# Two chains of two heads in place of one chain of four, in the gated recurrence of block 2

## The chip, the cores and the metric

The kernel runs on one core of a Trainium2 chip. The metric is the device time of one execution in microseconds (us), the median over runs. Engines are named as in the profile: PE is TensorE's matmuls, PEld its weight loads, DVE is VectorE, ACT is ScalarE, POOL is GpSimd, SP the engine whose queue issues the plain DMAs.

## The reference

One sequence of 256 tokens, width 1024, float32. First two "hybrid" layers (block 1), then two layers of block 2, each made of a feed-forward part, a mixer and a second feed-forward part, all with RMS norms and residuals. The mixer of block 2 has a forgetting attention (4 heads), a dilated attention (4 heads) and a gated linear recurrence (HGRN, 4 heads with 128 key and 128 value channels each), whose outputs are concatenated and projected by `w_out_2`. The change touches only the recurrence. For one head, with forget gate f between 0 and 1 per key channel, key k = 1 - f, query q (a SiLU of its projection) and value v:

```python
S[t] = diag(f[t]) @ S[t-1] + outer(k[t], v[t])     # 128 x 128 state
o[t] = S[t].T @ q[t]
y    = rmsnorm(o) * silu(gate)                     # gate: the hg columns
```

so that o[t] is the sum over s <= t of v[s] times the sum over channels of q[t] k[s] exp(sum of log f over s+1..t).

## The kernel before

**Layout.** Activations are kept with channels on partitions and the 256 tokens in the free dimension. The dense products are done in three terms: each weight chunk (128 x 2048 float32, 1 MB) is loaded to a tile `st` by SP's queue (`weight_loads`, line 600), its rounded part `hi` is made on ScalarE and the remainder `lo` on VectorE, or on ScalarE and a GpSimd accumulating DMA (`weight_splits`, line 617); a dense group of 256 output columns (`dense_t`, line 660) is then 48 matmuls of 128 x 256. There are three tiles each of `st`, `hi` and `lo`.

**Order.** No loop order is written by hand. Every piece of work is a generator that yields operations; at build time the `Scheduler` (lines 258 to 397) keeps one modelled clock per engine and always issues the operation with the smallest (modelled start - priority x weight). Each engine then runs its instructions in that fixed order. A generator that yields a tuple of tags waits until tiles of those tags are free: `lev` (3 tiles), `u` (3), `sm` (4 PSUM banks), `acc` (4 PSUM banks for dense groups). Priorities are in `PRIO`: attention 1.8, recurrence 2.3, a level's products 0.3, evacuation of dense groups 1.1. The model gives a ScalarE operation on SBUF 0.093 us plus 0.833 ns per column (line 454).

**The mixer of block 2** (`mix_b`, line 1370) runs twice. Dense groups follow `ORDER_B` (line 35): after the values `hi`, they are fv, hf0, hq0, hf1, fk, hq1, fq, dv, dk, dq, hg0, hg1. A digit 0 or 1 means heads 0 and 1, or heads 2 and 3. `hf` and `hq` evacuate a group into `sp` (running sums of log f, two halves of 1024 columns: prefix and suffix sides) and `kq` (keys and queries); `log1p_exp` (line 1403) is their common part and works in a `lev` tile. `hg` does the same for the output gate, then waits for the event `o0` or `o1` of its two heads and writes K blocks 4 and 5 (heads 0, 1) or 6 and 7 (heads 2, 3) of the projection's input.

**The recurrence** (`recurrence`, line 1512) is done without a loop over tokens. It waits for hf0, hf1, hq0 and hq1, takes the diagonal, and then goes through eight levels m = 1, 2, 4, ... 128. At each level ScalarE exponentiates the mixed halves of `sp` into a `lev` tile (1024 columns: 4 heads x 256 tokens), VectorE doubles the span of the running sums (two adds of 512 columns, line 1527 and 1528; not at the last level), and a spawned `level` task multiplies by `kq`, takes an `sm` bank, runs 64-column products on TensorE (`blocks`, line 1461) and merges them by a predicated copy into `at` (line 1489), or by ScalarE copies for the upper levels. Levels merge in order. After the eighth, for heads 0, 1 and then 2, 3: products of the values with `at`, square, product with ones for the norm, logarithm, and the event `o0` or `o1`.

**The projection** (`out_proj`, line 731): four banks are open at once. For each of the first four column blocks it runs K blocks 0 to 5, then K blocks 6 and 7 of the four (`LATE_B = 2`, `OPEN = 4`); the last four column blocks run straight through. K blocks 0 and 1 are the forgetting attention, 2 and 3 the dilated one. One K block is a pair: a 512-column matmul (line 576) and a 256-column one (line 577). An attention half (`heads`, line 963) takes two `sm` banks at once and there are two halves.

Of the kernel before, what the change touches and what calls it, by code (L numbers as in the profile page):

```python
# [17 lines left out]
P = 128  # L18
# [381 lines left out]
class Builder:  # L400
# [969 lines left out]
    def mix_b(self, l, st, nxt):  # L1370
        nc, tc, s = self.nc, self.tc, self.s
        done = Event()
        with tc.tile_pool(name="mixb", bufs=1, reuse_waits="tile") as mp:
# [29 lines left out]
            def log1p_exp(ps, nch, cols=None):  # L1403

                e = yield ("lev",)
                a = e[:, :nch * 512].rearrange("p (n f t) -> p n f t", n=nch, f=2)
                yield self.A(a[:, 0], ps, AF.Abs)
                if nch == 2:
                    for j in range(2):
                        yield self.A(a[:, 1, j], ps[:, j], AF.Abs, bias=cols[:, j:j + 1])  # L1410
                flat = e[:, :nch * 512]
                yield self.A(flat, flat, AF.Exp, scale=-1.0)
                yield self.A(flat, flat, AF.Ln, bias=1.0)
                return e, a

            def hf(c):
                def f_(bank, ps):
                    yield self.bconsts
                    h0 = 4 * l + 2 * c
                    e, a = yield from log1p_exp(ps, 2, self.nlncol[:, h0:h0 + 2])  # L1420
                    u, t1 = yield ("u", "u")
                    yield self.stt(u, ps, 0.0, a[:, 0], ALU.max, ALU.add)
                    yield self.stt(t1, ps, 0.0, a[:, 0], ALU.min, ALU.subtract)
                    for j in range(2):
                        h = 2 * c + j
# [5 lines left out]
                    yield self.V("tensor_tensor", u, u, a[:, 1], op=ALU.subtract)  # L1431
                    s.put("lev", e)
                    yield self.V("tensor_tensor", sp_[:, 1, c * 512:c * 512 + 512].rearrange("p (a b) -> p a b", a=2),
                                  t1, u, op=ALU.subtract)
                    s.put("u", u)
                    s.put("u", t1)
                    E[f"hf{c}"].done = True
                return f_

            def hq(c):  # L1440
                def f_(bank, ps):
                    e, a = yield from log1p_exp(ps, 1)
                    u = yield ("u",)
                    yield self.stt(u, ps, 0.0, a[:, 0], ALU.min, ALU.subtract)
                    s.put("lev", e)
                    yield self.A(u, u, AF.Exp)
                    yield self.tt(kq[:, 1, c * 512:c * 512 + 512].rearrange("p (a b) -> p a b", a=2), ps, u, ALU.mult)
                    s.put("u", u)
                    s.put("acc", bank)
                    E[f"hq{c}"].done = True  # L1450
                return f_

            def mixed(tl, m):

                return bass.AP(tensor=tl.tensor, offset=tl.offset,
                               ap=[list(tl.ap[0]), [2 * m, D // (2 * m)], [D + m, 2], [1, m]])

            b8 = lambda bank: bank.rearrange("p (h t) -> p h t", h=8)
            atc = at[:, 2].rearrange("p h (b j) -> p (h b) j", b=2)

            def blocks(bank, t, left, right):

                ops = []
                for h in range(4):
                    for b in range(2):
                        q = slice(h * T + t * P + 64 * b, h * T + t * P + 64 * b + 64)
                        ops.append((b8(bank)[64 * b:64 * b + 64, 4 * t + h], left[:, q], right[:, q], True, True))
                return self.MMs(ops)

            def diagonal():  # L1470
                bank = yield ("sm",)
                for t in range(2):
                    yield blocks(bank, t, kq[:, 0], kq[:, 1])
                yield self.tt(atc, b8(bank), self.c["identc"][:, None, :].to_broadcast([P, 8, 64]), ALU.mult)
                s.put("sm", bank)
                box["lev"] = [Event() for _ in range(9)]
                box["lev"][0].done = True

            def level(lev, e):
                m = 1 << lev  # L1480
                ev = e.rearrange("p (b two m) -> p b two m", two=2, m=m)
                yield self.V("tensor_tensor", ev, ev, mixed(kq, m), op=ALU.mult)
                bank = yield ("sm",)
                if m < 64:
                    for t in range(2):
                        yield blocks(bank, t, e, e)
                    yield box["lev"][lev]
                    mk = self.msk[:, lev * 64:lev * 64 + 64][:, None, :].to_broadcast([P, 8, 64])
                    yield Op([("V", .602, lambda: self.nc.vector.copy_predicated(atc, mk, b8(bank)))],
                             [extent(atc)], [extent(bank), extent(self.msk)])  # L1490
                    if m == 32:
                        for b in range(2):
                            bs = slice(64 * b, 64 * b + 64)
                            yield self.A(at[bs, 0:2, :, bs], atc[bs].rearrange("p (t h) j -> p t h j", t=2), AF.Copy)
                elif m == 64:
                    for h in range(4):
                        yield self.MMs([(b8(bank)[64 * t:64 * t + 64, h], e[:, h * T + t * P:h * T + t * P + 64],
                                         e[:, h * T + t * P + 64:h * T + t * P + P], True, True) for t in range(2)])
                    yield box["lev"][lev]
                    for t in range(2):  # L1500
                        yield self.A(at[:64, t, :, 64:], b8(bank)[64 * t:64 * t + 64, :4], AF.Copy)
                else:
                    pa = bank.rearrange("p (h t) -> p h t", h=4)
                    for h in range(4):
                        yield self.MM(pa[:, h], e[:, h * T:h * T + P], e[:, h * T + P:h * T + T])
                    yield box["lev"][lev]
                    yield self.A(at[:, 2], pa, AF.Copy)
                s.put("sm", bank)
                s.put("lev", e)
                box["lev"][lev + 1].done = True  # L1510

            def recurrence():

                for n in ("hf0", "hf1", "hq0", "hq1", "S0"):
                    yield E[n]
                yield from diagonal()
                for lev in range(8):
# [3 lines left out]
                    yield self.A(ev, mixed(sp_, m), AF.Exp)  # L1521
                    s.spawn(level(lev, e), PRIO["level"])
                    if m < 128:
                        sl = sp_[:, 0].rearrange("p (b two m) -> p b two m", two=2, m=m)
                        pl = sp_[:, 1].rearrange("p (b two m) -> p b two m", two=2, m=m)
                        n = D // (2 * m)
                        yield self.tt(sl[:, :, 0], sl[:, :, 0], pl[:, :, 1, m - 1:m].to_broadcast([P, n, m]), ALU.add)
                        yield self.tt(pl[:, :, 1], pl[:, :, 1], pl[:, :, 0, m - 1:m].to_broadcast([P, n, m]), ALU.add)
                yield box["lev"][8]
                for c in range(2):  # L1530
                    bank, sq = yield ("sm", "u")
                    po = bank.rearrange("p (a t) -> p a t", a=2)
                    for j in range(2):
                        h = 2 * c + j
                        vs = slice(h * P, h * P + P)
                        yield self.MM(po[:, j, :P], hv[:, 0, vs], at[:, 0, h])
                        yield self.MM(po[:, j, P:], hv[:, 0, vs], at[:, 2, h], True, False)
                        yield self.MM(po[:, j, P:], hv[:, 1, vs], at[:, 1, h], False, True)
                    yield self.A(sq, po, AF.Square)
                    yield self.A(oh[:, 2 * c:2 * c + 2], po, AF.Copy)  # L1540
                    yield self.MM(po, self.ones, sq)
                    s.put("u", sq)
                    yield self.A(lr[:, 2 * c:2 * c + 2], po, AF.Ln, scale=1.0 / P, bias=self.epsc)
                    s.put("sm", bank)
                    E[f"o{c}"].done = True
# [98 lines left out]
            def hg(c):  # L1644
                def f_(bank, ps):
                    e, a = yield from log1p_exp(ps, 1)
                    w = yield ("u",)
                    yield self.stt(w, ps, 0.0, a[:, 0], ALU.min, ALU.subtract)
# [52 lines left out]
            s.spawn(recurrence(), PRIO["rec"])  # L1701
# [195 lines left out]
```

## Time and profile before

| | us |
|---|---|
| median of 3 runs | 1345.81 (1343.68 to 1347.51) |
| profiled execution | 1343.41 |
| its span, first to last instruction | 1341.6 |
| PE busy | 1278.4 (95%) |
| ACT busy | 920.5 (69%) |
| DVE busy | 853.3 (64%) |
| mean granted clock of TensorE | 0.978 of full speed |

The first mixer's recurrence lies between about 497 and 600 us of the span, the second's between about 1018 and 1122. A busy PE is not PE at its peak, since matmuls are pipelined and their recorded durations overlap; the distance from start to start is what a matmul occupies.

### The profile page before, as it was taken

Reading aid. Unit: us, or ns where it says so; the run is one execution under the profiler, and the core shown is the slowest. Engines: PE = TensorE matmul, PEld = TensorE weight load, DVE = VectorE, ACT = ScalarE, POOL = GpSimd, SP = SyncE. Lnnn points to the kernel's source line nnn. Section 1 sums busy time; section 2 is a strip of 40 time slices with the busy share of each in tenths; the row PEclk is TensorE's granted clock in tenths of the full one; section 3 lists DMA queues with packets and bytes.
Section 4 is the critical chain, followed back from the end, with each engine's and each line's share of the span. In section 5 each row is a group of like instructions: output and inputs, shape, how many; then the busy total and the mean of one; then the engine's idle time right before and its main releaser. Section 6 shows DMA issues by size and latency. Waiting matters only on the chain.

```text
span 1341.6 us, 21822 instructions
## 1 busy us (share of the span) xinstructions
PE 1278.4 (95%) x8530; PEld 1140.2 (85%) x8530; DVE 853.3 (64%) x1561; ACT 920.5 (69%) x1422; POOL 212.0 (16%) x230
## 2 busy tenths in 40 slices
PE   6899889999999999979999999999999988999997
PEld 6888889888888899868888888888899877888886
DVE  6776678679775556946766556655555874665642
ACT  6487767785885579867766556666558885766652
POOL 3111111122111021001222102222011100122200
PEclk9899999999999999989999999999999997999998
DMA  8988998797777788628777787777778753887872
GB/s 272 239 216 236 237 260 257 191 259 216 226 234 224 234 246 248 169 92 223 226 229 234 227 238 220 234 229 228 230 234 247 215 172 96 218 236 221 255 224 76
DMA packets 59783, 294.09 MB, mean 219 GB/s; under 512 B 12448, under 2 KB 14240, under 8 KB 34208
## 3 DMA queue, kind: packets, MB, share of 16 engines
q1 hardware_dynamic: 39232, 219.01, 47.8%
q0 software_dynamic: 20448, 73.69, 28.4%
q8 instruction: 67, 1.10, 0.3%
q14 instruction: 36, 0.29, 0.1%
HBM read 217.94 MB, written 1.05 MB: 163 GB/s over the span
## 4 chain that ended last, share of the span: by engine, by line
PE 38%; DMA 29%; ACT 16%; DVE 10%; issue 6%; SPq 1%; POOL 0%; DVEq 0%; POOLq 0%; ACTq 0%
DMA st<-ws 15%; PE bank L576 14%; DMA lo<-st 14%; PE bank L577 8%; ACT hi L472 6%; DVE lo L495 3%; ACT lo L472 3%; PE bank L563 3%; PE bank L565 3%; PE bank L564 3%; PE bank L535 2%; PE bank L546 2%; ACT lev L472 2%; PE bank L579 1%; PE bank L553 1%
## 5 line engine op out<-in xcount | busy, mean ns | idle before, releaser
L576 PE MATMUL bank<-act,hi 128*128 128x512 f32 x1456 | 523.3, 397 | 2.7 <-DVE act L495 2.7
L472 ACT ACTIVATE hi<-st 128x1024 fp32r<-128x1024 f32 (+3 forms) x416 | 427.7, 1035 | 129.8 <-DMA st<-ws 119.0
L577 PE MATMUL bank<-act,lo 128*128 128x256 f32 x1664 | 436.3, 282 | 2.5 <-DMA lo<-st 2.5
L495 DVE TENSOR_TENSOR lo<-st,hi 128x1024 fp32r<-128x1024 f32 (+1 forms) x274 | 330.7, 1212 | 166.2 <-ACT hi L472 162.9
L577 PEld LDWEIGHTS bank<-act,lo 128*128 128x128 f32 x1664 | 314.5, 189 | 24.6 <-DMA lo<-st 6.9
L576 PEld LDWEIGHTS bank<-act,hi 128*128 128x128 f32 x1456 | 275.1, 189 | 57.6 <-DVE act L495 4.5
L592 POOL DMA_DIRECT2D lo<-st x142 | 123.1, 867 | 870.0 <-ACT lo L472 573.1
L576 PE MATMUL bank<-ha,hi 128*128 128x512 f32 x672 | 237.1, 394 | 0.0
L565 PE MATMUL bank<-act,lo 128*128 128x256 f32 x720 | 206.9, 287 | 19.9 <-DMA lo<-st 19.8
L563 PE MATMUL bank<-act,hi 128*128 128x256 f32 x720 | 211.4, 294 | 0.0
L564 PE MATMUL bank<-act,hi 128*128 128x256 f32 x720 | 205.3, 285 | 0.0
L577 PE MATMUL bank<-ha,lo 128*128 128x256 f32 x704 | 193.4, 282 | 1.3 <-DMA lo<-st 0.9
L565 PEld LDWEIGHTS bank<-act,lo 128*128 128x128 f32 x720 | 139.1, 193 | 21.5 <-DMA lo<-st 21.5
L472 ACT ACTIVATE lo<-hi 128x1024 fp32r<-128x1024 f32 (+1 forms) x142 | 149.2, 1051 | 3.8
L576 PEld LDWEIGHTS bank<-ha,hi 128*128 128x128 f32 x672 | 126.3, 188 | 26.8
L563 PEld LDWEIGHTS bank<-act,hi 128*128 128x128 f32 x720 | 139.5, 194 | 5.0 <-issue 4.5
L564 PEld LDWEIGHTS bank<-act,hi 128*128 128x128 f32 x720 | 138.9, 193 | 0.1
L577 PEld LDWEIGHTS bank<-ha,lo 128*128 128x128 f32 x704 | 132.3, 188 | 6.3 <-DMA lo<-st 3.6
L495 POOL TENSOR_TENSOR fs<-fs,rbc 128x512 f32<-128x512 f32 x44 | 64.1, 1457 | 179.8 <-ACT fs L472 179.8
L495 DVE SCALAR_TENSOR_TENSOR x<-bank,x 128x256 f32<-128x256 f32 x128 | 53.6, 422 | 44.9 <-PE bank L579 42.9
L579 PE MATMUL bank<-act,hi 128*128 128x512 f32 x208 | 82.0, 394 | 0.0
L495 DVE TENSOR_TENSOR fh<-bank,fh 128x256 f32<-128x256 f32 x88 | 36.8, 420 | 59.8 <-ACT fh L472 59.6
(214 smaller groups left out, 1437.0 us busy)
## 6 DMA issues: line engine op xcount, KB each, us to landing
st<-ws SPq DMA_DIRECT2D x197, 1024.0 KB, 5.8
lo<-st POOLq DMA_DIRECT2D x136, 512.0 KB, 7.8
st<-ws SPq DMA_DIRECT2D x2, 1040.0 KB, 8.5
st<-ws SPq DMA_DIRECT2D x4, 512.0 KB, 5.5
st<-ws SPq DMA_DIRECT2D x8, 192.0 KB, 5.2
nb<-rpb SPq DMA_DIRECT2D x16, 96.0 KB, 8.5
st<-ws SPq DMA_DIRECT2D x2, 768.0 KB, 7.3
lo<-st POOLq DMA_DIRECT2D x2, 520.0 KB, 10.1
```

The source lines that it names most:

```text
L472: return Op([("A", dur, lambda: self.nc.scalar.activation(out, in_, func, **kw))], outs, ins, ACT_SETS.get(func))
L495: return (eng, dur, lambda: fn(out, *ins, **kw)), [extent(a) for a in aps]
L535: return Op([("P", dur, lambda: self.nc.tensor.matmul(out, lhsT, rhs, start=start, stop=stop))], [extent(out)], [extent(lhsT), extent(rhs)])
L546: mm(o, l, r, start=st, stop=sp)
L553: return Op([("P", .11, lambda: self.nc.tensor.transpose(out, in_, ident))], [extent(out)], [extent(in_), extent(ident)])
L563: mm(out, ah, bh, start=first, stop=False)
L564: mm(out, ah, bl, start=False, stop=False)
L565: mm(out, al, bh, start=False, stop=last)
L576: mm(out, wh, x, start=first, stop=False)
L577: mm(out[:, 0], wl, x[:, 0], start=False, stop=False)
L579: mm(out, wh, x, start=False, stop=True)
L592: return Op([("G", ADD_ISSUE, lambda: self.nc.gpsimd.dma_start(out, src, accum_op=ALU.add))], [extent(out)], [extent(src), extent(out)], l ...
```

## The change

The recurrence becomes a task per pair of heads: `recurrence(c)` waits for `hf{c}`, `hq{c}` and the cleared tiles only, runs its diagonal and eight levels on 512 columns, and then does the products with the values of its own two heads and sets `o{c}`. Both tasks have the priority that the one had. The tiles `lev` become six of 512 columns in place of three of 1024. `log1p_exp` works on 512 columns; `hf` calls it twice in sequence (first for the gate's two softplus terms and the keys, then with the shifted bias), where it had one call on 1024 columns. The merge by predicated copy and the copies into `at` cover half the columns each; the modelled duration of the predicated copy is set to 0.385 us from 0.602.

```diff
-            for tag, n, shape in (("lev", 3, [P, D]), ("u", 3, [P, 2, T]), ("av", 2, [P, 2, T]), ("aq", 1, [P, 2, T]),
+            for tag, n, shape in (("lev", 6, [P, D // 2]), ("u", 3, [P, 2, T]), ("av", 2, [P, 2, T]), ("aq", 1, [P, 2, T]),
...
-                    e, a = yield from log1p_exp(ps, 2, self.nlncol[:, h0:h0 + 2])
+                    e, a = yield from log1p_exp(ps)
                     u, t1 = yield ("u", "u")
-                    yield self.stt(u, ps, 0.0, a[:, 0], ALU.max, ALU.add)
-                    yield self.stt(t1, ps, 0.0, a[:, 0], ALU.min, ALU.subtract)
+                    yield self.stt(u, ps, 0.0, a, ALU.max, ALU.add)
+                    yield self.stt(t1, ps, 0.0, a, ALU.min, ALU.subtract)
+                    s.put("lev", e)
                     for j in range(2):
                         h = 2 * c + j
                         yield self.A(kq[:, 0, h * T:h * T + T], u[:, j], AF.Exp, scale=-1.0,
                                      bias=self.l1mcol[:, h0 + j:h0 + j + 1])
+                    e, a = yield from log1p_exp(ps, self.nlncol[:, h0:h0 + 2])
...
-            def mixed(tl, m):
+            def mixed(tl, c, m):
+                n = D // 2
+                return bass.AP(tensor=tl.tensor, offset=tl.offset + c * n,
+                               ap=[list(tl.ap[0]), [2 * m, n // (2 * m)], [D + m, 2], [1, m]])
...
-                for h in range(4):
+                for h in range(2):
                     for b in range(2):
...
-                    mk = self.msk[:, lev * 64:lev * 64 + 64][:, None, :].to_broadcast([P, 8, 64])
-                    yield Op([("V", .602, lambda: self.nc.vector.copy_predicated(atc, mk, b8(bank)))],
-                             [extent(atc)], [extent(bank), extent(self.msk)])
+                    mk = self.msk[:, lev * 64:lev * 64 + 64][:, None, :].to_broadcast([P, 4, 64])
+                    yield Op([("V", .385, lambda: self.nc.vector.copy_predicated(atc[c], mk, b4(bank)))],
+                             [extent(atc[c])], [extent(bank[:, :T]), extent(self.msk)])
...
-            def recurrence():
-                for n in ("hf0", "hf1", "hq0", "hq1", "S0"):
+            def recurrence(c):
+                for n in (f"hf{c}", f"hq{c}", "S0"):
                     yield E[n]
-                yield from diagonal()
+                yield from diagonal(c)
+                half = D // 2
                 for lev in range(8):
                     m = 1 << lev
                     e = yield ("lev",)
                     ev = e.rearrange("p (b two m) -> p b two m", two=2, m=m)
-                    yield self.A(ev, mixed(sp_, m), AF.Exp)
-                    s.spawn(level(lev, e), PRIO["level"])
+                    yield self.A(ev, mixed(sp_, c, m), AF.Exp)
+                    s.spawn(level(c, lev, e), PRIO["level"])
...
-                yield box["lev"][8]
-                for c in range(2):
-                    bank, sq = yield ("sm", "u")
...
+                yield box["lev", c][8]
+                bank, sq = yield ("sm", "u")
...
-            s.spawn(recurrence(), PRIO["rec"])
+            for c in range(2):
+                s.spawn(recurrence(c), PRIO["rec"])
```

## Rows read from the trace of the kernel before

**Rows 1.** The page, busy time of the whole span.
```profile
PE 1278.4 (95%) x8530; PEld 1140.2 (85%) x8530; DVE 853.3 (64%) x1561; ACT 920.5 (69%) x1422; POOL 212.0 (16%) x230
```
**Rows 2.** Windows, first mixer: length, then PE, PEld, DVE, ACT, POOL busy; clock; DMA.
```profile
510.00:520.00 10.00, 10.00 (x87) 10.00 (x85) 5.71 (x8) 9.87 (x14) 0.94 (x2) 1.00 0.93 230
...
528.00:577.00 49.00, 46.02 (x556) 42.52 (x557) 41.59 (x95) 41.01 (x86) 4.31 (x5) 1.00 0.67 184
...
580.00:590.00 10.00, 4.76 (x22) 3.98 (x22) 3.62 (x4) 6.81 (x12) 0.00 (x0) 0.67 0.40 149
590.00:600.00 10.00, 7.28 (x28) 5.03 (x28) 3.98 (x9) 4.75 (x9) 0.00 (x0) 0.82 0.00 0
```
**Rows 3.** Windows, second mixer, same columns.
```profile
1110.00:1120.00 10.00, 7.51 (x19) 4.64 (x19) 3.03 (x6) 4.22 (x9) 0.00 (x0) 0.50 0.00 0
```
**Rows 4.** Timeline of PE, first mixer: start, length, what, idle before it.
```profile
577.59 0.39 PE L576 MATMUL bank<-act,hi 128*128 128x512 f32 x1
...
577.94 0.39 PE L576 MATMUL bank<-act,hi 128*128 128x512 f32 x1
...
578.79 0.69 PE L546 MATMUL bank<-lev 128*64 128x64 f32 x16
...
579.93 1.16 PE L535 MATMUL bank<-lev 128*128 128x128 f32 x8
...
584.92 0.79 PE L535 MATMUL bank<-at,hv 128*128 128x128 f32 x2 [3.83 <-ACT at L472]
...
595.28 1.13 PE L535 MATMUL bank<-u,ones 128*128 128x512 f32 x2 [1.23 <-ACT kq L472]
...
596.05 0.60 PE L576 MATMUL bank<-act,hi 128*128 128x512 f32 x1
...
598.25 0.50 PE L576 MATMUL bank<-act,hi 128*128 128x512 f32 x1 [1.49 <-DVE act L495]
```
**Rows 5.** Timeline of PE, second mixer.
```profile
1098.02 0.39 PE L576 MATMUL bank<-act,hi 128*128 128x512 f32 x1
...
1119.84 0.79 PE L576 MATMUL bank<-act,hi 128*128 128x512 f32 x1 [1.20 <-DVE act L495]
...
1123.01 0.40 PE L576 MATMUL bank<-act,hi 128*128 128x512 f32 x1
```
**Rows 6.** Timeline of DVE and ACT, first mixer.
```profile
508.99 0.69 DVE L495 TENSOR_TENSOR kq<-bank,u 128x512 f32<-128x512 f32 x1 [0.77 <-ACT u L472]
...
527.85 0.68 DVE L495 TENSOR_TENSOR kq<-bank,u 128x512 f32<-128x512 f32 x1
...
554.65 1.04 ACT L472 ACTIVATE lev<-sp 128x1024 f32<-128x1024 f32 x1
...
573.29 1.06 ACT L472 ACTIVATE lev<-sp 128x1024 f32<-128x1024 f32 x1 [0.54 <-PE bank L546]
...
575.72 0.42 DVE L495 TENSOR_TENSOR act<-bank,act 128x256 fp32r<-128x256 f32 x1
...
579.93 0.60 ACT L472 ACTIVATE lev<-bank 128x512 f32<-128x512 f32 x1
```
**Rows 7.** Tiles lev, sp, at: operation, count of both mixers, ns min/median/max, first and last.
```profile
L472 ACT ACTIVATE lev<-lev x24: 629/632/1063, 500.0 to 1104.4; 128x512 f32<-128x512 f32 x16, 128x1024 f32<-128x1024 f32 x8
L472 ACT ACTIVATE lev<-sp x16: 1044/1060/1530, 530.6 to 1096.3; 128x1024 f32<-128x1024 f32 x16
L495 DVE TENSOR_TENSOR lev<-lev,kq x16: 1210/1218/1534, 539.7 to 1099.1; 128x1024 f32<-128x1024 f32 x16
...
L495 DVE TENSOR_TENSOR sp<-sp x28: 684/693/694, 532.1 to 1095.5; 128x512 f32<-128x512 f32 x28
...
L1489 DVE COPY_PREDICATED at<-msk,bank x12: 730/740/756, 544.9 to 1097.3; 128x512 f32<-128x512 uint8 x12
...
L472 ACT ACTIVATE at<-at x4: 627/632/634, 577.7 to 1099.7; 64x512 f32<-64x512 f32 x4
```
**Rows 8.** Waits of PE's weight loads, 470 to 620 us: total, times, longest.
```profile
PEld bank L546 <- DVE lev L495: 0.3, 1, 0.3
```

More of the change, by code (lines that the diff above doesn't have):

```diff
@@ L1430, in f_ @@
                     s.put("acc", bank)
-                    yield self.V("tensor_tensor", u, u, a[:, 1], op=ALU.subtract)
+                    yield self.V("tensor_tensor", u, u, a, op=ALU.subtract)
                     s.put("lev", e)
@@ L1441, in f_ @@
                 def f_(bank, ps):
-                    e, a = yield from log1p_exp(ps, 1)
+                    e, a = yield from log1p_exp(ps)
                     u = yield ("u",)
-                    yield self.stt(u, ps, 0.0, a[:, 0], ALU.min, ALU.subtract)
+                    yield self.stt(u, ps, 0.0, a, ALU.min, ALU.subtract)
                     s.put("lev", e)
@@ L1451, in hq @@
                 return f_
-            def mixed(tl, m):
[L1455 to L1459, printed above, removed]
+            def mixed(tl, c, m):
+                n = D // 2
+                return bass.AP(tensor=tl.tensor, offset=tl.offset + c * n,
+                               ap=[list(tl.ap[0]), [2 * m, n // (2 * m)], [D + m, 2], [1, m]])
@@ L1461, in blocks @@
+            b4 = lambda bank: bank[:, :T].rearrange("p (h j) -> p h j", h=4)
+            atc = [at[:, 2, 2 * c:2 * c + 2].rearrange("p h (b j) -> p (h b) j", b=2) for c in range(2)]
             def blocks(bank, t, left, right):
                 ops = []
-                for h in range(4):
+                for h in range(2):
                     for b in range(2):
                         q = slice(h * T + t * P + 64 * b, h * T + t * P + 64 * b + 64)
-                        ops.append((b8(bank)[64 * b:64 * b + 64, 4 * t + h], left[:, q], right[:, q], True, True))
+                        ops.append((b4(bank)[64 * b:64 * b + 64, 2 * t + h], left[:, q], right[:, q], True, True))
@@ L1468, in blocks, with diagonal @@
                 return self.MMs(ops)
-            def diagonal():
+            def diagonal(c):
                 bank = yield ("sm",)
+                cs = slice(c * 512, c * 512 + 512)
                 for t in range(2):
-                    yield blocks(bank, t, kq[:, 0], kq[:, 1])
-                yield self.tt(atc, b8(bank), self.c["identc"][:, None, :].to_broadcast([P, 8, 64]), ALU.mult)
+                    yield blocks(bank, t, kq[:, 0, cs], kq[:, 1, cs])
+                yield self.tt(atc[c], b4(bank), self.c["identc"][:, None, :].to_broadcast([P, 4, 64]), ALU.mult)
@@ L1475, in diagonal, with level @@
                 s.put("sm", bank)
-                box["lev"] = [Event() for _ in range(9)]
-                box["lev"][0].done = True
-            def level(lev, e):
+                box["lev", c] = [Event() for _ in range(9)]
+                box["lev", c][0].done = True
+            def level(c, lev, e):
                 m = 1 << lev
+                hs = slice(2 * c, 2 * c + 2)
                 ev = e.rearrange("p (b two m) -> p b two m", two=2, m=m)
-                yield self.V("tensor_tensor", ev, ev, mixed(kq, m), op=ALU.mult)
+                yield self.V("tensor_tensor", ev, ev, mixed(kq, c, m), op=ALU.mult)
@@ L1483, in level @@
                 bank = yield ("sm",)
+                before = box["lev", c][lev]
                 if m < 64:
@@ L1520, in recurrence @@
                     ev = e.rearrange("p (b two m) -> p b two m", two=2, m=m)
-                    yield self.A(ev, mixed(sp_, m), AF.Exp)
-                    s.spawn(level(lev, e), PRIO["level"])
+                    yield self.A(ev, mixed(sp_, c, m), AF.Exp)
+                    s.spawn(level(c, lev, e), PRIO["level"])
                     if m < 128:
-                        sl = sp_[:, 0].rearrange("p (b two m) -> p b two m", two=2, m=m)
-                        pl = sp_[:, 1].rearrange("p (b two m) -> p b two m", two=2, m=m)
-                        n = D // (2 * m)
+                        sl, pl = (sp_[:, i, c * half:c * half + half].rearrange("p (b two m) -> p b two m", two=2, m=m)
+                                  for i in range(2))
+                        n = half // (2 * m)
@@ new lines, in recurrence @@
+                yield box["lev", c][8]
+                bank, sq = yield ("sm", "u")
+                po = bank.rearrange("p (a t) -> p a t", a=2)
+                for j in range(2):
+                    h = 2 * c + j
+                    vs = slice(h * P, h * P + P)
+                    yield self.MM(po[:, j, :P], hv[:, 0, vs], at[:, 0, h])
+                    yield self.MM(po[:, j, P:], hv[:, 0, vs], at[:, 2, h], True, False)
+                    yield self.MM(po[:, j, P:], hv[:, 1, vs], at[:, 1, h], False, True)
@@ L1547, in direct @@
+                yield self.A(sq, po, AF.Square)
+                yield self.A(oh[:, 2 * c:2 * c + 2], po, AF.Copy)
+                yield self.MM(po, self.ones, sq)
+                s.put("u", sq)
+                yield self.A(lr[:, 2 * c:2 * c + 2], po, AF.Ln, scale=1.0 / P, bias=self.epsc)
+                s.put("sm", bank)
+                E[f"o{c}"].done = True
             def direct(k):
@@ L1645, in f_ @@
                 def f_(bank, ps):
-                    e, a = yield from log1p_exp(ps, 1)
+                    e, a = yield from log1p_exp(ps)
                     w = yield ("u",)
-                    yield self.stt(w, ps, 0.0, a[:, 0], ALU.min, ALU.subtract)
+                    yield self.stt(w, ps, 0.0, a, ALU.min, ALU.subtract)
                     s.put("acc", bank)
```

52 lines of the change are left out of this document (19 added, 33 removed).

## The prediction

> **What bounds the kernel now.** I read the busy line of the page first, then busy time by windows inside the two gated mixers, then the order of TensorE's instructions where a window is poor, then who waits for whom. TensorE is busy 95% of the span [rows 1], so time can come back only where it stands still or runs slow. In the first mixer it is full at 510 to 520 us and busy 46.02 of the 49 us from 528 to 577; between 580 and 600 it is busy 4.76 and 7.28 of 10 us, at a granted clock of 0.67 and 0.82 [rows 2]. The second mixer has the same hole; its window 1110 to 1120 has a clock of 0.50, the lower of the two levels (1.2 of 2.4 GHz) nearly all along [rows 3].
>
> What the hole is made of [rows 4]: at 577.59 the output projection begins, runs four pairs of matmuls 0.35 us apart (the first four K blocks of its first column block, two of them around other work) and then needs K block 4, which is heads 0 and 1 of the recurrence. These come last: two level products (0.69 and 1.16 us), 3.83 us of waiting for ScalarE's copies into `at`, the products of `at` with the values, the square, the product with ones (after a 1.23 us wait), logarithm, gate, split. K block 4 arrives at 596.05, K block 5 at 598.25; only from there does TensorE run through. The second mixer: 1098.02 to 1119.84, and the five pairs from there to 1123.01 are still slow [rows 5].
>
> Why the recurrence is so late [rows 6]: heads 0 and 1 have their inputs at 509.7 (`hq0` ends), but the one chain over four heads begins only when `hq1` ends, at 528.5. Its sixth exponential is at 554.65, its seventh at 573.29, released by a level product on TensorE: the three `lev` tiles were all held by levels that had no PSUM bank of tag `sm`, since the dilated attention had taken two banks for each of its two halves (the last of its outputs is written at 576.1). The gate `hg0`, whose matmuls are done about a dense group (48 matmuls) before `hg1`, also asks for a `lev` tile, and gets its first step on ScalarE at 579.93.
>
> **The change, part by part.** *Earlier start and end of heads 0 and 1.* Their chain may begin at 509.7 instead of 528.5, 18.8 us sooner. One step of the chain is exponential, two adds, next exponential: today 1.060 + 2 x 0.693 us, halved 0.632 + 2 x 0.42 = 1.5 us [rows 6, 7] (0.42 is the 128x256 tensor_tensor of 575.72). Six of the eight steps, some 9 us plus hand-offs and the queueing of a full ScalarE, fit ahead of 528. With their last levels in the stretch 541 to 561, where no attention holds all four banks, `o0` should be done before 570, and `hg0` finds a `lev` tile (six instead of three). K blocks 4 and 5 are then there when the projection wants them.
>
> What that is worth: from the first pair to K block 5 is 598.25 - 577.59 = 20.66 us. Work in it that stays, at full clock: five pairs x 0.35 = 1.75; level products 0.69 + 1.16; 24 products of `at`, at 1.16 / 8 = 0.145 each, 3.48; two products with ones, 2 x 1.13 = 2.26; sum 9.3 [rows 4]. So 11.3 us is idle or slow clock. In the second mixer 21.82 - 9.3 = 12.5, and the slow pairs add 3.17 - 1.75 = 1.4: 13.9 [rows 5]. Together 25.2 us can come back. The 9.3 us of work is not saved; it moves, partly into stretches where TensorE is full.
>
> *What is late next.* After `hg1`'s last matmul its own gate needs ScalarE 3 x 0.63, VectorE 0.69 twice, exponential 0.63, scaling and split 3 x 0.42 (as the 128x256 operation at 575.72), about 5.2 us [rows 6, 7] and the hand-offs between the engines, for which I allow 2 us: about 7 us. Before K blocks 6 and 7 are needed the projection has four column blocks x six K blocks = 24 pairs, 8.4 us. That covers it if chain 1 is done; chain 1 begins at 528.5 as now, with half the work. Bounds of what stays idle: 0 (cover holds) to 9 us a mixer (TensorE stands as long as it does now, less the 24 pairs). I take 3, since weight splits of 1024 columns, about as long as the 1.060 of an exponential, stand between on ScalarE: 6 us in all.
>
> *More instructions.* Each halved operation pays its fixed part twice [rows 7]. ScalarE a mixer: eight exponentials 8 x (2 x 0.632 - 1.060) = 1.6; two `hf` evacuations, each 2 x 1.06 becoming 4 x 0.632, 0.8 together; the five copies into `at`, at most 0.632 each, between 0 and 3.2, taken as a fifth of it, 0.6 (the exponentials grow by a fifth): 3.0. VectorE: eight products 8 x (2 x 0.693 - 1.218) = 1.3; 14 adds 14 x (2 x 0.42 - 0.693) = 2.1; six predicated copies of 256 columns, not in the trace, between half and the whole of 0.740, taken as 0.740 - (0.693 - 0.42) = 0.47, so 1.2 (0 to 4.4); the diagonal 0.15: 4.7. TensorE issues the same matmuls as before, in smaller groups. No DMA is added. These 7.7 us lie on two engines beside TensorE; they cost only where TensorE waits for them. VectorE has room early on: 5.71 of 10 busy at 510 to 520. ScalarE hasn't: 9.87 there [rows 2], and it also makes the weight halves for TensorE. What chain 0 puts there (up to six exponentials, 3.8 us, and the `hf` extra) delays weight splits. Cover: chain 0's own products stand in the same stretch on TensorE (seven groups of 16 at 0.69 us or less [rows 4], up to 4.8 us, in which it needs no weights), and the splits run up to two groups ahead (three `hi` tiles). Bounds 0 to 4 us a mixer; I take 1: 2 us.
>
> The Trainium skill, "Perfetto Trace Analysis", section Optimizing Scalar/DVE Operations, gives a rule on both sides: grouping larger operations helps on a saturated engine, breaking them up lets work finish sooner on an engine that isn't saturated but holds others up. By it ScalarE at 510 to 520 speaks against this change and the hole at 580 to 600 for it; the first half is rival B.
>
> *Accumulator banks.* `hf` holds its bank through four exponentials and logarithms of 0.632 in place of two of 1.060, 0.4 us more, which would cost that much if a dense group waited for it; four such banks rotate over dense groups of 48 matmuls, so I take nothing.
>
> **The sum.** 25.2 - 6 - 2 = 17.2 us. The profiled execution took 1343.41 us (span 1341.6), 2.4 below the median 1345.81 of the runs; 1343.4 - 17.2 = 1326.2 there, 1328.6 against the median. I forecast 1329.
>
> **Rivals.**
> A. Chain 1 isn't earlier: attention takes the four `sm` banks as now, its last levels stay at 577 to 580 [rows 6], and the copies into `at` end when they do now. From 584.92: 12 x 0.145 of products, 0.6 for the square, 1.13, logarithm 0.6, gate and split 0.69 + 0.63 + 3 x 0.42, hand-offs 2, together 593.6, and 1 us more for the last of the copies; the 24 pairs end at 577.59 + 1.85 + 8.4 = 587.8, so TensorE stands 7 us. 25.2 - 2 x (7 + 1) = 9 us gained, 1337. For it: the banks and the priorities are the same, and now two chains ask. Against: it has half the work, and VectorE is freed of chain 0.
> B. ScalarE has no room: 4 us a mixer of chain 0's work show as waits for `lo` or `hi` between 510 and 545. 25.2 - 2 x (3 + 4) = 11 us, 1335. For it the 9.87 of 10; against it the work on TensorE that comes along.
> C. Attention becomes the last. It needs two banks at once, levels take one each as they come free; the dilated outputs, at 576.1 now [rows 6], are needed by the very first pairs. Late by 9 us, they eat the gain: 1346. Against: they have been ready 1.4 us before use, and attention's priority is unchanged.
> D. Slower. The order on each engine is fixed at build time by modelled durations, in which an exponential costs 0.09 us plus its columns, 0.946 for 1024 and 0.52 for 512, against 1.060 and 0.632 measured [rows 7]. With twice the instructions, each 0.11 longer than planned, TensorE's queue reaches a level's product before its data. There are 18 such steps a mixer (two diagonals, 16 levels), 36 in all; if each stops TensorE 1.2 us, as the ones product is stopped now [rows 4], that is 43 us, less 17: 26 slower, 1372. It decides from 17.2 / 36 = 0.48 us a step. Against: today TensorE's weight loads waited 0.3 us, once, for a level's factor between 470 and 620 us [rows 8], because dense matmuls stand between.
>
> **How the numbers follow.** Forecast 0.55, A 0.13, B 0.10, C 0.09, D 0.13. A difference under 0.3% (4 us) is what a measurement here can't tell from none. Faster: the forecast, A and B, 0.78; same: C, 0.09; slower: D, 0.13. The forecast's own range: 25.2 with nothing given back, and TensorE's idle 3 us a mixer between 528 and 577 also gone, 31 us, 1314; and 25.2 - 2 x (9 + 1) = 5, 1341. A and B lie inside. D and half of C are left out, with a little room: 1313 to 1345.
>
> **What would show it.** Right: exponentials of chain 0 from about 510 and, 520.4 us on (1098.02 less 577.59), 1030 us; `kq<-bank` copies of heads 0 and 1 before 575; no 10 us window under 8 busy or below clock 0.95 at 577 to 600 and 1098 to 1123; the projection's pairs unbroken up to the 24th. A wait before K block 6 is the 3 us, above 6 us rival A. Waits of TensorE for weight halves at 510 to 545 are B, for `act` in the projection's first four pairs C, for `lev` or `kq` anywhere D. Wrong: the hole as wide as now, or as much idle time opened ahead of it.

## The result, and the profile after

The changed kernel takes 1325.0 us (median of 4 runs, 1320.1 to 1329.4), the kernel before 1346.7 in the same group: ratio 0.984, 95% interval 0.980 to 0.988. In a second group, on one chip with other kernels, it was 1327.1 against 1346.0, ratio 0.9841 (0.9805 to 0.9877). The forecast was 1329, a gain of 17.2 us; measured are 21.7 and 18.9. Ratios are given as on record for each group; the quotient of the two medians can differ from them by up to 0.004 (for late, below, 1335.2 to 1347.8 is 0.991, on record 0.9943).

The profiled execution took 1320.14 us. Its busy lines, to hold against [rows 1]:

```profile
span 1318.3 us, 21934 instructions
...
PE 1270.8 (96%) x8530; PEld 1137.4 (86%) x8530; DVE 863.4 (65%) x1619; ACT 926.4 (70%) x1456; POOL 212.4 (16%) x230
```

VectorE has 10.1 us more work and ScalarE 5.9, TensorE the same instructions. The windows of [rows 2] and, last, of [rows 3]; columns: start:end, length, busy PE, PEld, DVE, ACT, POOL, then clock, share of the DMA engines, GB/s:

```profile
510.00:520.00 10.00, 9.27 (x107) 8.59 (x107) 7.38 (x13) 8.87 (x14) 0.86 (x1) 1.00 0.66 197
528.00:577.00 49.00, 46.78 (x514) 42.17 (x514) 39.54 (x94) 43.66 (x89) 5.16 (x6) 1.00 0.65 178
580.00:590.00 10.00, 10.00 (x80) 8.16 (x81) 5.63 (x20) 9.54 (x28) 0.86 (x1) 1.00 0.40 127
590.00:600.00 10.00, 8.40 (x53) 7.25 (x54) 6.32 (x10) 7.16 (x11) 0.86 (x1) 1.00 0.80 256
...
1110.00:1120.00 10.00, 10.00 (x59) 8.81 (x58) 8.72 (x22) 9.61 (x17) 1.72 (x2) 1.00 0.66 174
```

The hole at 580 to 600 is gone, and with it the low clock: 1.00 in place of 0.67, 0.82 and 0.50. The timeline of TensorE where the projection begins, to hold against [rows 4 and 5]: start, length, what, and in brackets the idle time before it:

```profile
587.97 0.48 PE L576 MATMUL bank<-act,hi 128*128 128x512 f32 x1
...
589.53 1.28 PE L546 MATMUL bank<-pt,av 128*64 128x128 f32 x12
592.40 0.50 PE L576 MATMUL bank<-act,hi 128*128 128x512 f32 x1 [1.60 <-DVE act L495]
...
1100.14 0.50 PE L576 MATMUL bank<-act,hi 128*128 128x512 f32 x1 [1.60 <-DVE act L495]
```

The pairs begin at 587.97, ten microseconds later than before (7.9 us counted from the start of the mixer), stop once, 1.60 us, behind the dilated attention's own last products (589.53), and then run through. The recurrence and the outputs, ScalarE and VectorE of the first mixer, against [rows 6]; the last line, apart, is of the kernel before:

```profile
513.62 0.85 ACT L472 ACTIVATE lev<-sp 128x512 f32<-128x512 f32 x1
516.13 0.71 ACT L472 ACTIVATE lev<-sp 128x512 f32<-128x512 f32 x1 [0.23 <-DVE sp L495]
517.80 0.63 ACT L472 ACTIVATE lev<-sp 128x512 f32<-128x512 f32 x1 [0.43 <-DVE sp L495]
...
546.27 0.86 ACT L472 ACTIVATE lev<-sp 128x512 f32<-128x512 f32 x1
...
551.85 0.67 ACT L472 ACTIVATE kq<-bank,epsc 128x512 f32<-128x512 f32 x1
...
578.00 0.59 ACT L472 ACTIVATE lev<-bank 128x512 f32<-128x512 f32 x1
...
581.47 0.69 ACT L472 ACTIVATE kq<-bank,epsc 128x512 f32<-128x512 f32 x1 [0.28 <-PE bank L535]
...
587.42 0.42 DVE L495 TENSOR_TENSOR act<-u,act 128x256 fp32r<-128x256 f32 x1
...
591.93 0.42 DVE L495 TENSOR_TENSOR act<-bank,act 128x256 fp32r<-128x256 f32 x1
```

```profile
591.74 0.69 ACT L472 ACTIVATE kq<-bank,epsc 128x512 f32<-128x512 f32 x1 [2.16 <-PE bank L535]
```

Chain 0's first three exponentials are at 513.62 to 517.80, chain 1's first at 546.27. Chain 0's last step, the logarithm at 551.85, sets `o0` at 552.5; before, the same step was at 591.74. K block 5 is written by 587.84 and K block 3, the second half of the dilated attention, by 592.35: it is now the last of the first six. The halved operations, tiles `at`, `lev` and `sp` of both mixers (columns as in [rows 7]):

```profile
L1495 DVE COPY_PREDICATED at<-msk,bank x24: 434/448/461, 522.4 to 1080.1; 128x256 f32<-128x256 uint8 x24
...
L472 ACT ACTIVATE lev<-sp x32: 617/632/860, 513.6 to 1070.4; 128x512 f32<-128x512 f32 x32
...
L495 DVE TENSOR_TENSOR sp<-sp x56: 415/425/428, 515.2 to 1066.1; 128x256 f32<-128x256 f32 x56
```

The table measures each mixer from its first value matmul to the start of the last matmul of its projection, in us, in one profiled execution of each kernel. The columns from "o0 set" to "pairs take" are the first mixer's: when `o0` is set, when VectorE has written K blocks 3 and 5, when the projection's first pair starts, all counted from the mixer's start, and how long the pairs take from there. after2 is the changed kernel and sm5b is sm5, each profiled a second time.

| kernel | o0 set | K block 3 | K block 5 | first pair | pairs take | mixer 1 | mixer 2 | ratio to before (95%) |
|---|---|---|---|---|---|---|---|---|
| before | 119.4 | 103.1 | 125.2 | 104.6 | 41.2 | 145.7 | 148.5 | 1 |
| changed | 77.0 | 116.8 | 112.3 | 112.5 | 25.6 | 138.1 | 136.3 | 0.984 (0.980 to 0.988) |
| after2 | 78.6 | 118.5 | 114.0 | 114.1 | 25.6 | 139.7 | 136.5 | 0.9841 (0.9805 to 0.9877) |
| late | 117.6 | 101.1 | 121.7 | 103.4 | 40.6 | 144.1 | 143.6 | 0.9943 (0.9912 to 0.9974) |
| serial | 80.5 | 115.6 | 113.2 | 110.3 | 33.5 | 143.7 | 140.2 | 0.9928 (0.9896 to 0.9961) |
| half4 | 105.5 | 120.5 | 110.9 | 112.8 | 30.4 | 143.2 | 145.2 | 0.993 (0.9894 to 0.9966) |
| hgx | 119.2 | 105.2 | 124.5 | 106.1 | 39.0 | 145.0 | 147.0 | 0.9972 (0.9947 to 0.9997) |
| korder | 78.6 | 118.4 | 113.9 | 114.0 | 24.7 | 138.7 | 135.8 | 0.9851 (0.9809 to 0.9893) |
| sm5 | 86.0 | 110.1 | 113.4 | 114.1 | 23.1 | 137.2 | 136.5 | 0.980 (0.9769 to 0.9832) |
| sm5b | 91.4 | 115.4 | 118.7 | 119.5 | 23.1 | 142.6 | 139.2 | 0.9814 (0.9768 to 0.9859) |
| bsm5 | 117.5 | 108.4 | about 123.6 | 111.4 | 33.7 | 145.1 | 144.1 | 0.9976 (0.9947 to 1.0004) |
| dbl | 93.9 | 130.7 | 127.1 | 120.2 | 32.0 | 152.2 | 152.4 | 1.0072 (1.0042 to 1.0102) |
| korder_b | 118.2 | 104.0 | 123.9 | 105.4 | 39.5 | 144.9 | 150.4 | 0.9997 (0.9967 to 1.0028) |
| dbl2 | 102.5 | 123.8 | 109.4 | 108.0 | 37.0 | 145.0 | 143.0 | 0.9976 (0.9945 to 1.0008) |

The two mixers give 294.2 - 274.4 = 19.8 of the 23.3 us by which the spans differ. All 64 pairs need 64 x 0.35 = 22.4 us: before they took 41.2 and 43.6, after 25.6 and 25.7. Two executions of one kernel show what a row is worth: "pairs take" repeats (25.6 and 25.6, 23.1 and 23.1), while the two mixers together differ by 1.8 us for the changed kernel and by 8.1 for sm5, all of it ahead of the first pair. So small differences of mixer lengths between kernels say little.

### The profile page after: what moved, and what is told of

It is laid out like the page before. It is cut to its first block, busy times and chain, and to the rows that moved or that the text cites. A ratio compares the mean times of both kernels' runs of the same rounds, so it can differ in the third digit from the quotient of the medians.

```text
span 1318.3 us, 21934 instructions
## 1 busy us (share of the span) xinstructions
PE 1270.8 (96%) x8530; PEld 1137.4 (86%) x8530; DVE 863.4 (65%) x1619; ACT 926.4 (70%) x1456; POOL 212.4 (16%) x230
## 4 chain that ended last, share of the span: by engine, by line
PE 60%; DMA 11%; issue 10%; ACT 9%; DVE 8%; SPq 0%; POOL 0%; POOLq 0%; DVEq 0%; ACTq 0%
PE bank L576 29%; PE bank L577 16%; DMA lo<-st 6%; DMA st<-ws 4%; PE bank L579 3%; ACT hi L472 3%; PE bank L563 2%; PE bank L565 2%; PE bank L564 2%; DVE lo L495 2%; PE bank L535 2%; PE bank L546 2%; ACT lo L472 1%; PE bank L553 1%; DVE ca L495 1%
## 5 line engine op out<-in xcount | busy, mean ns | idle before, releaser
L565 PEld LDWEIGHTS bank<-act,lo 128*128 128x128 f32 x720 | 140.0, 194 | 21.7 <-DMA lo<-st 21.7
```

The source lines that it names most:

```text
L565: mm(out, al, bh, start=False, stop=last)
```

## The experiments

**late**: both chains wait for all inputs.

```diff
-                for n in (f"hf{c}", f"hq{c}", "S0"):
+                for n in ("hf0", "hf1", "hq0", "hq1", "S0"):
```

> The changed kernel, but each of its two chains waits for hf0, hf1, hq0 and hq1, as the single chain did. Theory (early start): the gain comes from heads 0 and 1 starting when hq0 is done, some 25 us before hq1 is; without that most of it goes, 1340 to 1350 us against 1346.7 before and 1325 for the change, and TensorE stands idle again ahead of the output projection. Rival (splitting itself): smaller steps, six half tiles and separate ends o0 and o1 bring the gain whenever the chains start; then it stays at 1320 to 1330.

Measured: 1335.2 us, between the two expectations; the kernel before had 1347.8 in this group. In the trace the pairs take 40.6 us, as before the change. TensorE and ScalarE of this kernel, first mixer:

```profile
578.04 0.39 PE L576 MATMUL bank<-act,hi 128*128 128x512 f32 x1
...
582.57 0.63 PE L546 MATMUL bank<-lev 128*64 128x64 f32 x14 [2.96 <-DVE lev L495]
...
594.04 1.18 PE L535 MATMUL bank<-at,hv 128*128 128x128 f32 x8 [1.15 <-ACT at L472]
...
591.50 0.69 ACT L472 ACTIVATE kq<-bank,epsc 128x512 f32<-128x512 f32 x1 [0.50 <-PE bank L535]
```

The projection begins and then stands while the levels end; `o0` comes at 592.2. So without the early start the hole is back. The kernel is still faster than the one before: by the ratio 0.57% of the 1.6% remains, about a third (0.3 to 0.9% by its interval), and the mixers of this one execution are 6.5 of 19.8 us shorter. Whether smaller steps, separate ends, the six tiles or the split of `hf` give that part, no run here separates.

**serial**: the second chain waits for the end of the first.

```diff
-                for n in (f"hf{c}", f"hq{c}", "S0"):
+                for n in (f"hf{c}", f"hq{c}", "S0") + (("o0",) if c else ()):
```

> The changed kernel, but the second chain also waits for the event o0, so that the two chains never overlap. Theory: what counts is that chain 0 is done early; chain 1 has some 8 us to spare (its o1 comes at 582.2 us, the gate that uses it only at 591.3), so 1321 to 1329, as the change. Rival (concurrency): two chains fill each other's waits; without the overlap chain 1 ends 6 to 8 us later in each mixer, 1337 to 1341.

Measured: 1336.0, just under the rival's range. ScalarE and TensorE of the first mixer:

```profile
549.41 0.67 ACT L472 ACTIVATE kq<-bank,epsc 128x512 f32<-128x512 f32 x1
549.98 0.86 ACT L472 ACTIVATE lev<-sp 128x512 f32<-128x512 f32 x1
...
564.99 0.61 ACT L472 ACTIVATE lev<-sp 128x512 f32<-128x512 f32 x1
...
585.53 0.41 ACT L472 ACTIVATE at<-at 64x256 f32<-64x256 f32 x1
...
592.97 0.67 ACT L472 ACTIVATE kq<-bank,epsc 128x512 f32<-128x512 f32 x1
...
597.21 0.50 PE L576 MATMUL bank<-act,hi 128*128 128x512 f32 x1 [2.05 <-DVE act L495]
```

Counted from the mixer's start (469.55), chain 1's first exponential comes at 80.4, in the changed kernel at 70.8 (546.27), 9.6 us later; its logarithm comes at 123.4 in place of 106.0, 17.4 us later. Its eight exponentials are issued by 564.99, but its first copy into `at` comes only at 585.53, after the dilated attention's work: a late chain loses more than its delay, and K block 6 holds up the pairs by 2.05 us. My 8 us of slack was wrong: it counted the chain's delay alone.

**half4**: four half tiles `lev` in place of six.

```diff
-            for tag, n, shape in (("lev", 6, [P, D // 2]),
+            for tag, n, shape in (("lev", 4, [P, D // 2]),
```

> The changed kernel with four half-size lev tiles in place of six (two thirds of the memory). Theory: the number of these tiles is not what gives the gain, 1321 to 1332. Rival (tiles): more of them let levels and gates run ahead; with four a good part of the gain goes, 1335 to 1345.

Measured: 1337.7, the rival's range. The logarithm of chain 0 in this kernel, and the pair that waits for K block 3:

```profile
582.74 0.69 ACT L472 ACTIVATE kq<-bank,epsc 128x512 f32<-128x512 f32 x1
...
598.48 0.63 PE L576 MATMUL bank<-act,hi 128*128 128x512 f32 x1 [1.84 <-DVE act L495]
```

Chain 0 starts early (first exponential at 516.6) and yet ends at 583.4, 28.5 us later against the mixer's start than with six tiles. But that isn't what costs: K block 5, which needs `o0`, is written at 110.9, before the first pair (112.8) and no later than with six tiles (112.3). The projection waits for K block 3, at 120.5. So the tiles count, as the rival said; in this trace it is the attention that comes late with fewer of them, not heads 0 and 1.

**hgx**: the kernel before, the gates in tiles of their own.

```diff
-                    e, a = yield from log1p_exp(ps, 1)
+                    e = yield ("xnt",)
+                    yield self.A(e, ps, AF.Abs)
+                    yield self.A(e, e, AF.Exp, scale=-1.0)
+                    yield self.A(e, e, AF.Ln, bias=1.0)
...
-                    s.put("lev", e)
+                    s.put("xnt", e)
```

> The kernel before, with the two output gates hg0 and hg1 working in tiles of their own (tag xnt, free at that time), so that they wait for no lev tile. Theory: the hole is set by the chain's end, o0, not by the gate; only the 2 to 3 us by which the gates hold ScalarE ahead of the copies into at come back in each mixer, 1339 to 1343. Rival (gate starved of its tile): most of the gain of the change comes from this, 1320 to 1330.

Measured: 1341.1, ratio 0.9972, in the theory's range. The gate's first step on ScalarE, which was at 579.93 [rows 6]:

```profile
565.87 0.60 ACT L472 ACTIVATE xnt<-bank 128x512 f32<-128x512 f32 x1
```

So the gate did wait for a `lev` tile, as read, but that was not what the projection waited for: `o0` stays at 119.2, and the pairs take 39.0 in place of 41.2.

**after2** is the changed kernel again:

> The changed kernel again, unaltered, so that it stands beside the other kernels of this group on one chip. Theory: ratio to before 0.980 to 0.989, as measured first.

Measured 0.9841, as given above.

**korder**: another order of K blocks.

```diff
-K_OUT_B = (0, 1, 2, 3, 4, 5, 6, 7)
+K_OUT_B = (0, 1, 4, 5, 2, 3, 6, 7)
-LATE_B = 2
+LATE_B = 4
```

> The changed kernel with the output projection of block 2 taking K blocks 0, 1, 4, 5 first for its four open column blocks and 2, 3, 6, 7 after (in place of 0 to 5, then 6, 7). In the changed kernel TensorE waits once in each mixer, 1.6 us, for K block 3, the last of the dilated attention, which has become the last of the first six. Theory: K blocks 4 and 5 are there by 588, the 16 pairs of the first part cover K block 3, and the two waits go: 3 us less than the changed kernel in the same group. Rival: another wait follows at once (K block 6 at 595), no change within 1 us.

Measured: 1326.3 against 1327.1 for the changed kernel in the group; the runs can't tell them apart, as the rival said. In the trace the 1.60 us wait is gone and one of 0.55 follows; the pairs take 24.7.

**sm5 and bsm5**: one accumulator bank lent to the `sm` banks from the values to the projection, in the changed kernel and in the one before.

```diff
+                lent = yield ("acc",)
+                s.put("sm", lent)
                 for key in ORDER_B:
...
+                lent = yield ("sm",)
+                s.put("acc", lent)
                 yield from self.out_proj("o", box["y"], KT, K_OUT_B, LATE_B, 1.0, nxt, yready)
```

> The changed kernel with one accumulator bank lent to the sm banks between the values and the output projection: five sm banks, three accumulator banks. Theory (the sm banks are what chains and attention fight for): K block 3 comes earlier and the wait of 1.6 us in each mixer goes, 2 to 6 us less than the changed kernel. Rival: dense groups wait for the third accumulator bank, 0 to 8 us more.

> The kernel before with the same loan: five sm banks. Theory: its one chain stood from the sixth to the seventh exponential (18.6 us) for want of an sm bank while the dilated attention held all four; with a fifth bank the levels go on, the chain ends 5 to 8 us sooner in each mixer and the hole shrinks by that, 1331 to 1339. Rival: VectorE's order, not the banks, held the chain; 1343 to 1350.

Measured: sm5 1321.6, 5.5 us under the changed kernel's 1327.1; bsm5 1341.7, 4.2 under before, its interval reaching 1. K block 3 of sm5 on VectorE and the pairs' start on TensorE, then, for bsm5, the seventh exponential and the logarithm of `o0`:

```profile
583.20 0.42 DVE L495 TENSOR_TENSOR act<-bank,act 128x256 fp32r<-128x256 f32 x1
...
587.70 0.48 PE L576 MATMUL bank<-act,hi 128*128 128x512 f32 x1
588.13 0.39 PE L576 MATMUL bank<-act,hi 128*128 128x512 f32 x1
```

```profile
567.75 1.04 ACT L472 ACTIVATE lev<-sp 128x1024 f32<-128x1024 f32 x1
...
589.98 0.69 ACT L472 ACTIVATE kq<-bank,epsc 128x512 f32<-128x512 f32 x1 [0.27 <-PE bank L535]
```

In sm5 K block 3 is there 4 us before the first pair and the wait is gone, as expected: the pairs take 23.1 us in place of 25.6, 5 us over both mixers. In bsm5 the seventh exponential moves from 573.29 to 567.75, so the levels had waited for the bank; but `o0` comes only 1.9 us sooner in the first mixer and 4.9 in the second (117.5 and 114.8, before 119.4 and 119.7). The other brake is VectorE's order, the rival: the factor of the fourth level, whose exponential was at 545.59 before and 548.24 in bsm5, is multiplied by `kq` only at 561.4 in both (the first line is the kernel before, the second bsm5):

```profile
561.42 1.22 DVE L495 TENSOR_TENSOR lev<-lev,kq 128x1024 f32<-128x1024 f32 x1
```

```profile
561.36 2.35 DVE L495 TENSOR_TENSOR lev<-lev,kq 128x1024 f32<-128x1024 f32 x2
```

The time lies between the two ranges, nearer to the rival's.

sm5 again, in another group:

> The changed kernel with the loan of one accumulator bank to the sm banks, once more, in another group of runs. Theory: ratio to before 0.977 to 0.983, below the 0.984 of the change; rival: it is the change's 0.984 with chance on its side, 0.983 to 0.988.

Measured: 1322.2, ratio 0.9814 (0.9768 to 0.9859). Both values lie under the change's, and the intervals overlap: sm5 is faster than the kernel before, and probably, not surely, faster than the changed one.

**dbl and dbl2**: exponentials issued twice, at all levels (20 us more of ScalarE work) and at two of eight (5 us).

```diff
                     yield self.A(ev, mixed(sp_, c, m), AF.Exp)
+                    yield self.A(ev, mixed(sp_, c, m), AF.Exp)
```

```diff
                     yield self.A(ev, mixed(sp_, c, m), AF.Exp)
+                    if lev in (1, 5):
+                        yield self.A(ev, mixed(sp_, c, m), AF.Exp)
```

The first edit is dbl's, the second dbl2's.

> The changed kernel with the exponential of every level issued twice (same input, same output): 16 more ScalarE instructions of 0.63 us in each mixer, 10 us each, 20 us in all, three times what the change itself adds to ScalarE. Theory: the added instructions lie beside TensorE's work and cost little, 0 to 6 us over the changed kernel, ratio to before 0.984 to 0.989. Rival (ScalarE has no room): each of them shows, 15 to 25 us over the changed kernel, no faster than before.

> The changed kernel with the exponential issued twice at two of the eight levels only: four more ScalarE instructions of 0.63 us in each mixer, 2.5 us each, 5 us in all, somewhat less than the 3.0 a mixer that the change itself was reckoned to add. All sixteen twice cost about 28 us for 20 us of work. Theory (a margin): small additions lie hidden until ScalarE's margin is used up, 0 to 2 us over the changed kernel, ratio to before 0.982 to 0.986. Rival (proportional): 1.4 us for each us, 7 us over it, ratio 0.988 to 0.991.

Measured: dbl 1355.3, ratio 1.0072; dbl2 1340.3, ratio 0.9976. Against the changed kernel's 1327.1, measured in another group, that is 28 us for 20 of work, and 13 for 5 (by the ratios 31 and 18): neither a margin nor a proportion. For dbl, the windows ahead of the old hole, and TensorE and ScalarE in them:

```profile
520.00:530.00 10.00, 10.00 (x118) 9.16 (x114) 8.38 (x20) 8.09 (x16) 0.00 (x0) 1.00 0.11 47
530.00:540.00 10.00, 3.31 (x45) 2.60 (x44) 7.96 (x15) 9.87 (x15) 0.86 (x1) 0.78 0.28 52
```

```profile
534.17 0.45 PE L546 MATMUL bank<-lev 128*64 128x64 f32 x8 [2.76 <-DVE lev L495]
...
540.94 1.12 PE L546 MATMUL bank<-lev 128*64 128x64 f32 x16 [3.50 <-DVE lev L495]
...
515.06 1.05 ACT L472 ACTIVATE hi<-st 128x1024 fp32r<-128x1024 f32 x1
...
533.85 1.04 ACT L472 ACTIVATE lo<-hi 128x1024 fp32r<-128x1024 f32 x1
```

Chain 0 takes ScalarE from the weight splits: there is none from 516.1 to 533.9, few weights are loaded meanwhile (DMA share 0.11 at 520 to 530, in the changed kernel 0.40), and TensorE, with no dense group between them, stands 2.76 and 3.50 us at level products whose data are late. The granted clock of that window is 0.78. For dbl2, TensorE, ScalarE and VectorE of the first mixer:

```profile
589.69 0.49 PE L535 MATMUL bank<-at,hv 128*128 128x128 f32 x2 [2.68 <-ACT at L472]
...
574.62 0.67 ACT L472 ACTIVATE kq<-bank,epsc 128x512 f32<-128x512 f32 x1
...
581.79 0.42 DVE L495 TENSOR_TENSOR act<-u,act 128x256 fp32r<-128x256 f32 x1
...
596.16 0.42 DVE L495 TENSOR_TENSOR act<-bank,act 128x256 fp32r<-128x256 f32 x1
```

K blocks 4 and 5 are in time (582.2, with the first pair at 580.83), but the order has come out another way: chain 1's value products stand in TensorE's queue ahead of the rest of the dilated attention and wait 2.68 us for their copies, and K block 3 is there only at 596.6.

**korder_b**: the kernel before with the first four K blocks of four column blocks ahead of the rest (`LATE_B = 4`).

> The kernel before, with the output projection of block 2 taking K blocks 0 to 3 first for its four open column blocks, then 4 to 7 (in place of 0 to 5, then 6, 7). Theory (the hole is idle time that any ready work fills): 12 more pairs of 0.35 us run inside the hole in each mixer, 4.2 us, and K blocks 4 to 7 are wanted later; 8 to 11 us less than before, ratio 0.992 to 0.994. Rival: the hole's length is set by something the pairs don't shorten, ratio 0.997 to 1.0.

Measured: 1345.1, ratio 0.9997, the rival. TensorE, first mixer:

```profile
601.50 0.80 PE L576 MATMUL bank<-act,hi 128*128 128x512 f32 x1 [0.90 <-DVE act L495]
...
604.18 0.80 PE L576 MATMUL bank<-act,hi 128*128 128x512 f32 x1 [1.68 <-DVE act L495]
```

All 16 early pairs run in the hole, but what follows wants K blocks 6 and 7 a little after 4 and 5, and K block 6 comes 2.7 us after K block 5: the pairs take 39.5 in place of 41.2. Work put into the hole doesn't make the chain end sooner. In the second mixer a late weight half cost 3.9 us more, and K block 3 came at 118.6 in place of 103.4.

## Why the prediction was right, point by point

- *Early start.* Chain 0 begins at 513.6 (said: about 510) and `o0` is set at 552.5 (said: before 570). late shows that the early start is needed: without it the hole is back. So early an end is not: half4 sets `o0` 28.5 us later and dbl2 25.5 us, and K block 5 is written at 110.9 and 109.4 all the same, in the changed kernel at 112.3. There K block 5 follows `hg0`'s own gate, whose first step is at 578.00, not `o0`.
- *What the hole is worth.* The prediction had 43.9 us from first pair to K block 5 and slow pairs, of which 9.3 a mixer is work that moves. In the trace the pairs take 15.6 and 17.9 us less, and begin 7.9 and 5.8 us later, since the moved work (the 9.3 less the five pairs, 7.6) now stands ahead of them: net 7.6 and 12.2 by the lengths of the mixers, 6.0 and 12.0 in the second profile. Less its deductions the forecast had 7.3 and 9.9. The 3.5 us by which the spans differ outside the mixers are in no term of it.
- *What is late next.* Wrong in the name, and half the size. I expected `hg1`'s gate and K blocks 6 and 7, 3 us a mixer. It is K block 3, rival C's mechanism, with 1.60 us in place of the 9 that rival needed; the sign "unbroken up to the 24th" fails at the fourth pair. Attention slips by 13.7 us against the mixer's start (103.1 to 116.8), the first pair by 7.9. Chain 1 doesn't begin "as now" either: its first exponential comes 70.8 us after the mixer's start, the one chain's came at 57.5. With half the work it still ends sooner (its logarithm at 106.0, before 123.4), so rival A's wait doesn't come.
- *More instructions.* Their durations were right: predicated copy 0.448 (said 0.47), ScalarE 5.9 us more over both mixers (said 6.0), VectorE 10.1 (said 9.4). "They cost only where TensorE waits for them" was no safe way to price them: dbl2 adds 5 us of ScalarE work, less than the change itself does, and loses 13 us. What their own price is stays open, since no kernel here has the early start without them. Rival D's waits stayed small: in the first mixer 0.73 us for `kq` (before, 0.70) and 0.50 for `lev`.
- *ScalarE full at 510 to 520* (rival B). One wait of 1.04 us for a weight half at 537.83 in the first mixer (2.29 in the second profile), 0.30 in the second mixer, against the 1 us a mixer that was deducted. dbl shows that the danger was real: there this mechanism and rival D's waits open a new hole.
- *The `sm` banks.* The reading of [rows 6], that the chain was late because attention held the banks, was too simple: with a fifth bank the old chain still ends 1.9 and 4.9 us sooner only, and VectorE multiplies the held levels' factors no earlier (bsm5).
- *Luck.* The prediction worked out which input is last, not the order that the build would give every queue. That this order came out well is luck in so far: late and serial change one line each, half4 one number, dbl2 two lines, and each loses, by the ratios, more than half of the gain.

The Trainium skill, "Perfetto Trace Analysis", section Optimizing Scalar/DVE Operations, says that breaking up instructions may let work be completed sooner where an engine isn't saturated but causes bubbles on others. The trace agrees in so far as the wait for ScalarE's copies, 3.83 us at 584.92, is gone. But late has the same small instructions, and its pairs still take 40.6 us: here it is the earlier start that closes the bubble, not the size of the steps alone. No run here shows the section's other half, that grouping can help a saturated engine: dbl adds instructions and groups none.

What stays open is how much of the 20 us belongs to the idea and how much to the order that the `Scheduler` happened to find. late, serial, half4 and dbl2 each differ in a line or two from the changed kernel and keep, by the ratios, 0.2 to 0.7% of its 1.6%. For each the trace names the K block that is late (4 and 5 in late, 6 in serial, 3 in half4 and dbl2); none shows that another order of the same work could not have had it in time.

## What to carry to other kernels

When an engine that should be full stands still, find the one input that comes last and ask when its own inputs were ready: here 18.8 us before the chain that used them began. Then list the arrival times of all inputs of that consumer, because the second latest becomes the bound, and compare it with the first use. Where a program orders the queues from modelled durations, as here, any edit can reshuffle them: four more ScalarE instructions a mixer undid most of a gain of 1.6%, so a variant is judged by its trace, not by the size of its edit. And before reading a few microseconds out of one trace, profile the same kernel twice: here two executions of one kernel differed by 8.1 us over the two mixers.

## What the runs showed of the hardware

An exponential of 512 columns took 0.85, 0.71 and 0.63 us at levels 1, 2 and 3 (513.62 to 517.80), whose operands are runs of 1, 2 and 4 columns in memory; on 1024 columns it was 1.53 at the first level against a median of 1.06 [rows 7]. So at 512 columns runs of one column cost 0.22 us more here, runs of two 0.08, and from runs of four on nothing changes. Halving a predicated copy took it from 0.740 to 0.448 us, not to half.
